# Half loads and an early split at the start, two reorderings in the MLP, and another inverse rms for the last rows, in a one-core transformer layer

## The chip, the cores and the metric

The kernel runs on one NeuronCore of a Trainium2 chip. Its engines are TensorE (PE, matrix products, with a separate weight load PEld), VectorE (DVE), ScalarE (ACT), GpSimd (POOL) and SyncE (SP), which issues the DMAs. Each engine works through its own instruction stream in order; semaphores tie them together. The metric is the device time in microseconds, lower is better. Before the change it is 1483.99 us (median of three runs, 1483.71 to 1484.88).

## The reference

One layer of an encoder on `x` of 1024 tokens by 1024 features, in float32. Each sub-layer is normalised on the way in and on the way out and added to the residual.

```
h = rmsnorm(x, g_mix_pre);  proj = h @ w_in
y = concat(rmsnorm(forgetting_attention(fq, fk, fv, f_logit)),
           rmsnorm(chunked_relpos_attention(cq, ck, cv, rel_bias)))     # 8 + 8 heads of 64
x = x + rmsnorm(y @ w_out, g_mix_post)
x = x + rmsnorm(memory_cross_attention(rmsnorm(x), rmsnorm(mem)), g_mem_post)   # 4 heads, 256 memory tokens
y = square(relu(rmsnorm(x, g_ff_pre) @ w_ff1)) @ w_ff2                  # hidden 4096
out = x + rmsnorm(y, g_ff_post)
rmsnorm(x, g) = x * rsqrt(mean(x*x) + 1e-6) * g
```

## The kernel before

Every float32 product is made of three products of fp32r parts: each operand is split into `hi` (a copy in fp32r, by ACT) and `lo` (the rest, by DVE or POOL), and `mm3` (lines 193 to 195) issues hi.hi, lo.hi and hi.lo into one PSUM bank. So an operand is ready for PE only when both parts are, and the second and third products wait for the lo parts.

**Start** (from line 1368, an order written out by hand). `xT` is the transposed input in pairs of 128-row slices; slice kc of 8 is scaled by the gain into `hT[0]` (`gained`: ACT makes hi, DVE makes lo). Two value weights are loaded in parts and split: weight 1 (`w1`, 256 columns, two parts of 4 slices) and weight 0 (`w0`, 264 columns, three parts of 3, 3 and 2). `wraw` has three buffers, so a fourth weight part waits for the first to be split. PE first runs 30 transposes of the identity as a warm-up, then 8 slices of weight 1 for four banks (96 matmuls: slice kc of all four banks, then the next kc), then eight small matmuls `ssx` that sum squares over the features, then blocks of weight 0, one bank at a time (24 matmuls each). `square` makes the squares on ACT and adds them on DVE. For the other half of the tokens ACT squares whole rows of `x` (`row_squares`). POOL takes the inverse roots by `pow` (`rcols`), and PE broadcasts them by the transposes `rr`. The order of the loads is that of SP's instruction stream.

**Attention and cross-attention** are ordered by a planner (`Flow`) with costs and due times; the change does not touch it.

**MLP** (from line 1700, again in a hand-written order). Both products are done as one level of a seven-product scheme (Strassen, Winograd's form). In the first half each j of 16 has the products `px`, `pz`, `px` again, `pv`, `pz` again; the weight sums for j + 1 are made on POOL (`nxt.sums`) and split on ACT and DVE (`nxt.split`). `g22` (line 1948) reads the bank `pz`, which the fifth product adds into, so PE waits there until DVE has made g22. `sums` (the function that line 1975 defines) squares and adds the results of one j and stores them to `gd` in DRAM. In the second half there are seven products n = 0 to 6 of 8 steps k each; `fetch(s)` loads the rows of step s, `prepare(s)` splits them (and, for some products, first adds or subtracts weights), and `multiply` runs 24 matmuls a step for four row blocks. The banks are X (n = 0, 2, 4, 6) and Y (n = 1, 3, 5). `gather` moves them to the row accumulators `yc`. After n = 4 ACT copies X to the first half of rows 4 to 7, and after n = 6 DVE subtracts the new X from it.

**End.** The last three steps of n = 6 run one row block at a time: `gather`, `squares` (ACT sums the squares of the half row; DVE multiplies by the gain), `inverse` (POOL: sum, then `pow`), and `finish` (DVE: scale and add the residual, in two halves, each stored by SP).

Of the kernel before, what the change touches and what calls it, by code (L numbers as in the profile page):

```python
# [14 lines left out]
F32 = mybir.dt.float32  # L15
# [120 lines left out]
def build(ctx, tc, nc, out, t):  # L136
# [127 lines left out]
    def load_pair(th, p):  # L264
# [3 lines left out]
        nc.sync.dma_start(xt, t["xT"][th, p])  # L268
        return xt
# [17 lines left out]
    def value_weights(g, raws=None, only=None):  # L287

        n = 264 if g == 0 else 256
        src = t["w_v0"] if g == 0 else t["w_v1"]  # L290
        raws = [] if raws is None else raws
        for i, (a, b) in enumerate(((0, 3), (3, 6), (6, 8)) if g == 0 else ((0, 4), (4, 8))):
            if only in (None, i):
                raw = wp.tile([P, b - a, n], F32, tag="wraw", bufs=3, name=f"wrawv{g}{a}")
                nc.sync.dma_start(raw, src[:, a:b, :])
                raws.append(raw)
        return raws

    def value_split(g, raw, i, pieces=1):
# [6 lines left out]
        for j in range(0, k, n):  # L306
            nc.scalar.activation(wh[:, j:j + n, :], raw[:, j:j + n, :], AF.Copy)
            nc.vector.tensor_sub(wl[:, j:j + n, :], raw[:, j:j + n, :], f(wh[:, j:j + n, :]))
        return [(wh[:, j, :], wl[:, j, :]) for j in range(k)]
# [1060 lines left out]
    with tc.manual_schedule():  # L1370
        xT = {0: [load_pair(0, 0)], 1: []}
        gmix = const.tile([P, KC], F32, name="gmix")
        nc.sync.dma_start(gmix, t["g_mix_pre"])
        raw1 = value_weights(1, None, 0)
        xT[0] += [load_pair(0, 1), load_pair(0, 2)]
        value_weights(1, raw1, 1)
        xT[0].append(load_pair(0, 3))
        raw0 = value_weights(0, None, 0)
        vs = {g: value_tiles(g) for g in (1, 0)}
        warm = mm_tile([P, 4, P], "warm", "tr")  # L1380
        for n in range(30):
            nc.tensor.transpose(warm[:, n % 4, :], ident, ident)

        def gained(kc):

            x, g, dh = xT[0][kc // 2][:, kc % 2, :], gmix[:, kc:kc + 1], hT[0].hi(kc)
            nc.scalar.activation(dh, x, AF.Copy, scale=g)
            nc.vector.scalar_tensor_tensor(hT[0].lo(kc), x, g, f(dh), op0=ALU.mult, op1=ALU.subtract)
# [11 lines left out]
        for kc in (0, 1):  # L1400
            gained(kc)
        w1 += value_split(1, raw1[0], 0, 2)
# [26 lines left out]
        w0 += value_split(0, raw0[1], 1)  # L1429
        nc.vector.tensor_scalar(rcols[0], ps, EPS, None, op0=ALU.add)  # L1430
        nc.gpsimd.tensor_tensor(rcols[0], rcols[0], mhalf[:, 0:4], op=ALU.pow)
        w0 += value_split(0, raw0[2], 2)

        def row(b):
            xr.append(p1.tile([P, D], F32, tag="sp", bufs=5, name=f"x{b}"))
            nc.sync.dma_start(xr[-1], t["x"][b * P:(b + 1) * P, :])
# [7 lines left out]
        for b in range(4, TB):  # L1444
            row(b)
        for p in range(4):
            xT[1].append(load_pair(1, p))
        ps0 = [values(0, w0, 0, "s")]
        for b in (4, 5):
            row_squares(b)  # L1450
        for kb in range(4):
            value_leave(1, kb, first[kb])
        for b in (6, 7):
            row_squares(b)
# [421 lines left out]
    def prepare(s):  # L1876
# [19 lines left out]
        elif name in ("T3", "T4"):  # L1896
            nc.vector.tensor_sub(rb, t2b[k], rb)
        nc.scalar.activation(ah, ra, AF.Copy)  # L1898
# [8 lines left out]
    with manual:  # L1907
        sums = lambda: None
        for j in range(NP):
# [38 lines left out]
            nc.vector.tensor_add(g22, z, u3)  # L1948
            if after:
# [37 lines left out]
        sums()  # L1987


        pfs.close()  # L1990
# [183 lines left out]
```

## Time and profile before

| | |
|---|---|
| median of the runs | 1483.99 us (1483.71 to 1484.88) |
| profiled execution, its own time | 1484.06 us |
| its span in the trace | 1482.3 us |
| PE busy | 1466.0 us, 99% |
| DVE, ACT, POOL busy | 948.6, 797.3, 391.3 us |
| DMA | 220.67 MB, mean 149 GB/s |
| granted TensorE clock, mean | 0.999 |

A row of a timeline gives start, length (both in us), engine, line, operation, what is written and read, the shape and the count; the bracket at its end is the time that the engine was idle before it and what ended that. A row of the waits names who waited for whom, the total in us, how often, and the longest. A row of a group has the count, then the busy time in us and the mean length of one in ns. A row of a DMA issue has its size and the time from issue to landing.

### The profile page before, as it was taken

What the parts mean: (1) busy time and instruction counts of PE and PEld (TensorE: products, weight loads), DVE (VectorE), ACT (ScalarE), POOL (GpSimd) and SP (SyncE); (2) the same over time, 40 slices, a digit from 0 to 9 for tenths busy, and PEclk for the clock granted to TensorE, in tenths of its full rate; (3) what the DMA queues carried; (4) which work ended last, traced back from release to release, by engine and by line L of the source; (5) the groups of instructions that cost most, each with busy time, mean ns of one, the idle gap of its engine ahead of it and who ended that gap; (6) DMA issues with size and microseconds to landing.
All of it is one profiled execution on the core that took longest, in us unless ns stands there. A gap on an engine that the chain in (4) does not pass through costs nothing. (4 is left out here: it accounts for less than half of the span.)

```text
span 1482.3 us, 21601 instructions
## 1 busy us (share of the span) xinstructions
PE 1466.0 (99%) x7606; PEld 1250.3 (84%) x7606; DVE 948.6 (64%) x1644; ACT 797.3 (54%) x1417; POOL 391.3 (26%) x613
## 2 busy tenths in 40 slices
PE   8999999999999999999999999999999999999998
PEld 8989888888889988888888887888888888888886
DVE  6777667565576835974384687675444665656577
ACT  6567567465567835553353455555555453443542
POOL 0144355353344200531041413432222000000021
PEclk9999999999999999999999999999999999999999
DMA  7133322522315552461251447674445785445565
GB/s 271 48 87 79 82 67 70 150 67 60 79 58 149 176 178 85 154 202 58 89 182 43 153 146 241 235 243 148 155 150 170 250 346 178 142 139 202 178 247 199
DMA packets 83484, 220.67 MB, mean 149 GB/s; under 512 B 10008, under 2 KB 14112, under 8 KB 83376
## 3 DMA queue, kind: packets, MB, share of 16 engines
q1 hardware_dynamic: 83376, 219.30, 44.6%
q8 instruction: 60, 0.98, 0.3%
q14 instruction: 48, 0.39, 0.1%
HBM read 159.96 MB, written 50.91 MB: 142 GB/s over the span
## 5 line engine op out<-in xcount | busy, mean ns | idle before, releaser
L700 DVE TENSOR_TENSOR pl<-ptr,ph 128x512 fp32r<-128x512 f32 (+1 forms) x152 | 92.2, 616 | 39.5 <-ACT ph L703 34.8
L1898 ACT ACTIVATE whif<-ra 128x1024 fp32r<-128x1024 f32 x37 | 39.2, 1061 | 122.1 <-PE fy L194 62.6
L1900 DVE TENSOR_TENSOR wlof<-ra,whif 128x1024 fp32r<-128x1024 f32 x37 | 45.3, 1225 | 91.2 <-ACT whif L1898 91.2
L703 ACT ACTIVATE ph<-ptr 128x512 fp32r<-128x512 f32 (+1 forms) x152 | 79.1, 539 | 39.4 <-PE ptr L694 32.9
L2014 POOL TENSOR_SCALAR rf<-sf 128x1 f32<-128x1 f32 x8 | 8.2, 1028 | 326.6 <-ACT jf L1999 326.3
L731 PE MATMUL pv<-ph,vs 128*128 128x256 f32 x304 | 79.6, 286 | 0.0
L732 PE MATMUL pv<-pl,vs 128*128 128x256 f32 x304 | 78.6, 283 | 0.3 <-DVE pl L700 0.3
L193 PE MATMUL fx<-vhif,whif 128*128 128x512 f32 x168 | 65.4, 389 | 0.0
L194 PE MATMUL fx<-vlof,whif 128*128 128x512 f32 x168 | 65.4, 389 | 0.0
L195 PE MATMUL fx<-vhif,wlof 128*128 128x512 f32 x168 | 65.4, 389 | 0.0
L732 PEld LDWEIGHTS pv<-pl,vs 128*128 128x128 f32 x304 | 57.6, 189 | 4.6 <-POOL pl L689 0.5
L731 PEld LDWEIGHTS pv<-ph,vs 128*128 128x128 f32 x304 | 57.3, 189 | 4.1
L1788 POOL TENSOR_TENSOR sc<-wf,wf 128x512 f32<-128x512 f32 x14 | 20.1, 1437 | 144.0 <-DMA wf<-in_w_ff 89.3
L193 PE MATMUL k<-hT_hi,whik 128*128 128x512 f32 x128 | 52.5, 411 | 0.0
L193 PE MATMUL mq<-h2T_hi,whimq 128*128 128x512 f32 x128 | 51.5, 403 | 0.0
L193 PE MATMUL q<-hT_hi,whiq 128*128 128x512 f32 x128 | 50.9, 398 | 0.0
L193 PE MATMUL ym<-whimo,oT_hi 128*128 128x512 f32 x128 | 50.3, 394 | 0.1
L194 PE MATMUL k<-hT_lo,whik 128*128 128x512 f32 x128 | 50.2, 393 | 0.0
L193 PE MATMUL yw<-whiwo,yT_hi 128*128 128x512 f32 x128 | 50.2, 392 | 0.0
L195 PE MATMUL k<-hT_hi,wlok 128*128 128x512 f32 x128 | 50.1, 392 | 0.0
L194 PE MATMUL q<-hT_lo,whiq 128*128 128x512 f32 x128 | 50.1, 391 | 0.0
L195 PE MATMUL mq<-h2T_hi,wlomq 128*128 128x512 f32 x128 | 50.1, 391 | 0.0
(606 smaller groups left out, 5027.1 us busy)
## 6 DMA issues: line engine op xcount, KB each, us to landing
ra<-gd SPq DMA_DIRECT2D x56, 512.0 KB, 3.9
wg<-in_w_ff SPq DMA_DIRECT2D x56, 512.0 KB, 5.9
wf<-in_w_ff SPq DMA_DIRECT2D x38, 512.0 KB, 4.0
gd<-s SPq DMA_DIRECT2D x48, 256.0 KB, 2.1
wrawmq<-in_w_mq SPq DMA_DIRECT2D x16, 512.0 KB, 3.8
wrawmo<-in_w_mo SPq DMA_DIRECT2D x16, 512.0 KB, 3.8
gd<-u SPq DMA_DIRECT2D x32, 256.0 KB, 2.1
gd<-g SPq DMA_DIRECT2D x25, 256.0 KB, 2.5
```

Source lines behind the costliest of these rows:

```text
L193: nc.tensor.matmul(ps, lh, rh, start=start, stop=False, skip_group_check=more)
L194: nc.tensor.matmul(ps, lh, rl, start=False, stop=False, skip_group_check=more)
L195: nc.tensor.matmul(ps, ll, rh, start=False, stop=stop, skip_group_check=more)
L700: flow.put("V", at, 0.7, lambda: nc.vector.tensor_sub(pl[:, live, :], tr[:, live, :], f(ph[:, live, :])), done)
L703: flow.put("S", flow.end, 0.6, lambda ph=ph, tr=tr, live=live: nc.scalar.activation(ph[:, live, :], tr[:, live, :], AF.Copy), split)
L731: nc.tensor.matmul(pv, v, ph[:, hs, :], start=c == 0 and half == 0, stop=False)
L732: nc.tensor.matmul(pv, v, pl[:, hs, :], start=False, stop=c + 1 == len(steps) and half == 1)
L1788: eng.tensor_sub(sc[:, k1], r0[:, k0], r1[:, k0])
L1898: nc.scalar.activation(ah, ra, AF.Copy)
L1900: nc.vector.tensor_sub(al, ra, f(ah))
L2014: nc.gpsimd.tensor_scalar(r, ssf[b][:, 0:1], ssf[b][:, 1:2], EPS, op0=ALU.add, op1=ALU.add)
```

## The change

- The first pair of `xT` and the first part of weight 1 are loaded in halves, in the order x half, gain, weight half, x half, weight half. A one-element activation (`early`) stands first on ACT, and the warm-up has 20 transposes in place of 30.
- The first part of weight 1 gets its hi parts from POOL; between its two halves stand the lo of slice 0 and both parts of slice 1.
- Weight 0's middle part gets a buffer of its own (tag `bias`); its last part is loaded behind rows 4 and 5 of `x`. Its first block is multiplied ahead of `ssx`, its middle split comes ahead of the last two squares, and all four row squares come ahead of the evictions of weight 1.
- The two value weights lie in DRAM part by part, so that a partition's values of one part are together.
- In the MLP's first half, for j = 0, the split of the next `s23` goes behind `g22`. `prepare(2)` goes ahead of the last `sums`, and these come at step 2 of the second half, behind `prepare(3)` and `prepare(4)`.
- T4's operands are swapped, and product 6 adds into the banks of products 0, 2 and 4; the copies and subtractions that this needed go. `squares` reads the bank.
- For row block 7, ACT takes a root q of the sum a (e = second half's sum + eps as its bias), and DVE makes 1 / (a / q + q), with a factor 2 in the gain. Its stores go out in two queues, 64 rows each (SP and ACT).

The core of the diff:

```diff
-        xT = {0: [load_pair(0, 0)], 1: []}
+        early = const.tile([P, 1], F32, name="early")
+        nc.scalar.activation(early, mhalf[:, 0:1], AF.Copy)
+        xt, xloads = load_pair(0, 0, True)
+        raw, wloads = value_raw(1, 0, halves=True)
+        xT, raw1 = {0: [xt], 1: []}, [raw]
         gmix = const.tile([P, KC], F32, name="gmix")
+        xloads[0]()
         nc.sync.dma_start(gmix, t["g_mix_pre"])
-        raw1 = value_weights(1, None, 0)
+        wloads[0]()
+        xloads[1]()
+        wloads[1]()
         xT[0] += [load_pair(0, 1), load_pair(0, 2)]
...
-        for n in range(30):
+        for n in range(20):
...
-        for kc in (0, 1):
-            gained(kc)
-        w1 += value_split(1, raw1[0], 0, 2)
+        gained_hi(0)
+        w1 += value_split(1, raw1[0], 0, 2, lambda: (gained_lo(0), gained(1)))
...
@@ value_split
+            if between:
+                nc.gpsimd.tensor_copy(wh[:, j:j + n, :], raw[:, j:j + n, :])
+            else:
+                nc.scalar.activation(wh[:, j:j + n, :], raw[:, j:j + n, :], AF.Copy)
             nc.vector.tensor_sub(wl[:, j:j + n, :], raw[:, j:j + n, :], f(wh[:, j:j + n, :]))
+            if between and j == 0:
+                between()
...
-        value_weights(0, raw0, 1)
-        value_weights(0, raw0, 2)
+        raw0 += [value_raw(0, 1, "bias"), None]
         for kc in (4, 5):
             square(kc)
         w0 += value_split(0, raw0[0], 0)
+        w0 += value_split(0, raw0[1], 1)
         for kc in (6, 7):
             square(kc)
+        for b in (4, 5):
+            row(b)
+        raw0[2] = value_raw(0, 2)
+        w0 += value_split(0, raw0[2], 2)
+        ps0 = [values(0, w0, 0, "s")]
...
@@ first half of the MLP
-                nxt.split("s23")
+                if j:
+                    nxt.split("s23")
...
             nc.vector.tensor_add(g22, z, u3)
+            if more and not j:
+                nxt.split("s23")
...
@@ between the halves
-        sums()
-        pfs.close()
+        prepare(2)
...
-                if s + 2 < len(steps):
+                if 0 < s < len(steps) - 2:
                     prepare(s + 2)
+                if s == 2:
+                    sums()
+                    pfs.close()
...
-                multiply(banks, range(4), [s], n in (2, 4, 5))
+                multiply(banks, range(4), [s], n in (2, 4, 5, 6))
...
@@ the last rows
+        def inverse_last(b):
+            a, q, r = (small.tile([P, 1], F32, tag="rstd", bufs=8, name=f"{k}f{b}") for k in "aqr")
+            e = small.tile([P, 1], F32, tag="rstd", bufs=8, name=f"ef{b}")
+            nc.vector.tensor_scalar(e, ssf[b][:, 1:2], EPS, None, op0=ALU.add)
+            nc.scalar.activation(q, e, AF.Sqrt)
+            yield
+            nc.scalar.activation(q, ssf[b][:, 0:1], AF.Sqrt, bias=e)
+            nc.gpsimd.tensor_scalar(a, ssf[b][:, 0:1], ssf[b][:, 1:2], EPS, op0=ALU.add, op1=ALU.add)
+            nc.vector.reciprocal(r, q)
+            nc.vector.scalar_tensor_tensor(q, a, r, q, op0=ALU.mult, op1=ALU.add)
+            nc.vector.reciprocal(r, q)
+            rf[b] = r
+            yield
...
-                nc.sync.dma_start(out[b * P:(b + 1) * P, cs], xts[b][:, cs])
+                if b < TB - 1:
+                    nc.sync.dma_start(out[b * P:(b + 1) * P, cs], xts[b][:, cs])
+                    continue
+                for i, queue in enumerate((nc.sync, nc.scalar)):
+                    r = slice(i * P // 2, (i + 1) * P // 2)
+                    queue.dma_start(out[b * P:(b + 1) * P, cs][r, :], xts[b][r, cs])
...
         for tp in range(4):
-            multiply(X, [tp], range(len(steps) - 3, len(steps)), False)
+            multiply(X, [tp], range(len(steps) - 3, len(steps)), True)
             if tp:
                 finish(tp + 3)
-            gather(6, tp, X[tp])
-            squares(tp + 4, 0, True)
-            inverse(tp + 4)
+            if tp == 3:
+                next(last)
+            squares(tp + 4, 0, X[tp])
+            if tp < 3:
+                inverse(tp + 4)
+        next(last)
         finish(7)
```

More of the change, by code (lines that the diff above doesn't have):

```diff
@@ L262, in build, with load_pair @@
     hT = [Act(f"hT{h}") for h in range(2)]
-    def load_pair(th, p):
+    def load_pair(th, p, halves=False):
         tag = "sp" if th else "klo"
         xt = p1.tile([P, 2, HT], F32, tag=tag, bufs=5 if th else 4, name=f"xT{th}{p}")
-        nc.sync.dma_start(xt, t["xT"][th, p])
-        return xt
+        if not halves:
+            nc.sync.dma_start(xt, t["xT"][th, p])
+            return xt
+        return xt, [lambda j=j: nc.sync.dma_start(xt[:, j, :], t["xT"][th, p][:, j, :]) for j in (0, 1)]
     rows = []
@@ L285, in build, with value_raw, value_split @@
     fcol = p1.tile([P, TB, 8], F32, tag="o2", bufs=2, name="fcol")
[L287 to L299, printed above, removed]
+    VPARTS = {1: ((0, 4), (4, 8)), 0: ((0, 3), (3, 6), (6, 8))}
+    def value_raw(g, i, tag=None, halves=False):
+        n, (a, b) = 264 if g == 0 else 256, VPARTS[g][i]
+        shape = [P, b - a, n]
+        raw = (wp.tile(shape, F32, tag="wraw", bufs=3, name=f"wrawv{g}{a}") if tag is None else
+               p1.tile(shape, F32, tag=tag, bufs=2, name=f"wrawv{g}{a}"))
+        src = t[f"w_v{g}"][a * P * n:b * P * n].rearrange("(p k n) -> p k n", p=P, n=n)
+        if not halves:
+            nc.sync.dma_start(raw, src)
+            return raw
+        h = (b - a) // 2
+        return raw, [lambda j=j: nc.sync.dma_start(raw[:, j:j + h, :], src[:, j:j + h, :]) for j in (0, h)]
+    def value_split(g, raw, i, pieces=1, between=None):
         k, shape = raw.shape[1], list(raw.shape)
@@ L1442, in row_squares @@
             nc.scalar.activation(junk, xr[b - 4], AF.Square, scale=1.0 / 32.0, accum_out=ss1[:, b - 4:b - 3])
-        for b in range(4, TB):
+        for b in (6, 7):
             row(b)
@@ L2129, in blocks, with parts @@
         return a(w.reshape(KC, P, -1, P).transpose(2, 1, 0, 3))
-    def rows(w):
-        return a(w.reshape(KC, P, -1).transpose(1, 0, 2))
+    def parts(w, ranges):
+        w = w.reshape(KC, P, -1)
+        return a(np.concatenate([w[x:y].transpose(1, 0, 2).reshape(-1) for x, y in ranges]))
     w = i["w_in"][0]
```

59 lines of the change are left out of this document (31 added, 28 removed).

## The prediction

> **What bounds the kernel now.** I read the page first (share of each engine), then the list of what TensorE (PE) waited for, then the timelines around those waits, and the last microseconds.
>
> ```profile
> span 1482.3 us, 21601 instructions
> PE 1466.0 (99%) x7606; PEld 1250.3 (84%) x7606; DVE 948.6 (64%) x1644; ACT 797.3 (54%) x1417; POOL 391.3 (26%) x613
> ```
>
> PE is busy for all but 16.3 us of the span, and the change leaves its arithmetic alone. What can be won lies in those 16 us; what can be lost is a new wait. The waits:
>
> ```profile
> PE v L193 <- ACT whiv L307: 2.7, 1, 2.7
> PE pz L193 <- DVE g L1948: 1.2, 1, 1.2
> PE rr L1464 <- POOL rx L1456: 1.0, 1, 1.0
> PE fx L194 <- DVE bl L1901: 0.7, 1, 0.7
> PE ssx L1428 <- DVE sqx L1397: 0.4, 1, 0.4
> ```
>
> The other long piece is the time after the last matmul. The diff touches each of these places, so I price three stretches: start, middle, end.
>
> **Start: half loads, first split on GpSimd (POOL).**
>
> ```profile
> 1.34 5.20 PE L1382 MATMUL warm<-ident 128*128 128x128 f32 x30 [1.34 <-POOL ident masks.py:199]
> 4.50 1.28 ACT L1387 ACT_TABLE_LOAD   x1 [4.50 <-DMA gmix<-in_g_mix_pre]
> 8.57 1.15 ACT L307 ACTIVATE whiv<-wrawv 128x512 fp32r<-128x512 f32 x2 [1.45 <-DMA wrawv<-in_w_v]
> 9.87 1.34 ACT L1387 ACTIVATE hT_hi<-xT,gmix 128x512 fp32r<-128x512 f32 x2
> 10.20 0.28 PE L195 MATMUL v<-whiv,hT_lo 128*128 128x256 f32 x1
> 14.23 1.29 DVE L308 TENSOR_TENSOR wlov<-wrawv,whiv 128x512 fp32r<-128x512 f32 x2
> 21.36 0.28 PE L195 MATMUL v<-whiv,hT_lo 128*128 128x256 f32 x1
> ```
>
> The first value phase has 96 matmuls (8 slices kc, 4 banks, 3 products). The third starts at 10.20 and the last at 21.36: 93 steps in 11.16 us, 0.12 each, with no gap. It starts late because the first value weight lands at about 8.5; ScalarE (ACT) then splits it.
>
> After the change a quarter as many bytes must land before the first multiplication can have both operands: half of x, the gain, half of the weight. That half weight lands somewhere between 4.5 (when gmix, issued before it, has landed) and 8.5 (when the whole one lands now). POOL's copy of 128x512 is not in this trace; the nearest row with one large input is wider, and its length is my price:
>
> ```profile
> L632 POOL TENSOR_SCALAR spc1g<-spc1g,smc1g 128x640 f32<-128x640 f32 x4 | 3.2, 802 | 4.9 <-DVE smc1g L631 4.8
> L436 POOL TENSOR_TENSOR wloq<-wrawq,whiq 128x512 fp32r<-128x512 f32 x16 | 20.6, 1308 | 34.6 <-ACT whiq L427 34.5
> ```
>
> So 0.8, upper end 1.3 (two inputs), lower end the 0.58 of one ACT copy (1.15 for two). Landing at 5.0 plus 0.1 plus 0.8, then VectorE (DVE) 0.69 for the low part and 0.75 for hT_lo(0): the third matmul would start near 7.3 instead of 10.2. The table load moves ahead of all this (the tiny "early" activation), and hides. Ten warm-up transposes fewer end PE's warm-up near 5.0 to 5.6; they cost nothing, as PE then waits anyway.
>
> But the gain is capped by the next load. xT1 is the whole second pair, behind the same bytes as now:
>
> ```profile
> 2.10 0.91 SPq L268 DMA_DIRECT2D xT<-in_xT  x2
> ...
> xT<-in_xT SPq DMA_DIRECT2D x1, 512.0 KB, 7.8
> wrawv<-in_w_v SPq DMA_DIRECT2D x1, 512.0 KB, 9.4
> wrawv<-in_w_v SPq DMA_DIRECT2D x1, 396.0 KB, 10.4
> ```
>
> Issued at 2.10, it lands 7.8 later, at 9.9, and ACT begins hT_hi(2) at 9.87 already now. From there ACT's and DVE's orders are unchanged as far as the low part of weight kc 4, which is ready at 14.23 + 0.69 = 14.92. PE's 50th matmul (first low product of kc 4) cannot start before 14.95; now it starts at 10.20 + 47 x 0.12 = 15.84. So the phase ends 0.9 earlier, not 2.9: it moves to the last matmul at 20.5.
>
> Second weight: its middle part gets the free "bias" buffer, so it loads at once; its last part goes behind two rows of x. The last two wrawv rows land at 3.04 + 9.4 and 4.32 + 10.4, so about 0.4 MB per us; the middle part lands near 15.7, two rows near 18.3, the last part near 19, before DVE wants it at 22.8. In the DVE order the two squares additions now follow the middle split:
>
> ```profile
> 20.45 1.48 DVE L1397 TENSOR_TENSOR sqx<-sqx,sqx 128x512 f32<-128x512 f32 x2
> 23.16 0.71 DVE L308 TENSOR_TENSOR wlov<-wrawv,whiv 128x528 fp32r<-128x528 f32 x1
> 23.33 1.43 POOL L1431 TENSOR_TENSOR rx<-rx,mhalf 128x4 f32<-128x4 f32 x1 [22.04 <-DVE rx L1430]
> 28.85 1.05 POOL L1456 TENSOR_TENSOR rx<-rx,mhalf 128x4 f32<-128x4 f32 x1
> 29.95 1.09 PE L1464 MATMUL rr<-ident,rx 128*128 128x128 f32 x8 [0.99 <-POOL rx L1456]
> ```
>
> DVE's work from 20.45 on is the same but for one tiny operation, so wlov's last part ends near 23.5. PE begins the second weight's first block at 20.6, reaches kc 6 at 22.8 and waits 0.7 there: a new stall in place of ssx's. The block ends at 24.1, ssx (eight small matmuls, priced like rr's, 1.0) at 25.1, the next block (24 x 0.12) at 28.0. POOL's roots keep their order: the first follows ssx as now, 25.5 to 26.9, the second one's addition and root to about 28.2 (ACT's four row squares, now ahead of the evictions, are in time). So rr starts near 28.25 instead of 29.95: **1.7 won**. Bounds: if the halves land no earlier than 8.5, the low part, hT_lo(0) and (1) and the other low part push DVE's chain 1.3 to 1.5 later and 0.2 stays; if xT1 too comes 1.4 earlier, 3.1. The four value evictions move behind rows 6 and 7's squares; PE needs their banks only after rr.
>
> **Middle: two reorderings.**
>
> ```profile
> 910.12 1.33 DVE L1586 TENSOR_TENSOR v1lo_s<-sc,v1hi_s 128x1024 fp32r<-128x1024 f32 x1 [4.91 <-ACT v1hi_s L1583]
> 912.09 0.69 DVE L1948 TENSOR_TENSOR g<-pz,u 128x512 f32<-128x512 f32 x1
> ...
> 908.59 0.39 PE L195 MATMUL px<-T_hi,v0lo_s 128*128 128x512 f32 x1
> 911.31 0.39 PE L195 MATMUL pv<-T_hi,wlo_s1a 128*128 128x512 f32 x1
> 912.93 0.47 PE L193 MATMUL pz<-B_hi,u0hi_s 128*128 128x512 f32 x1 [1.24 <-DVE g L1948]
> ```
>
> DVE sat 4.91 waiting for v1hi_s (late through its load and POOL) with g22's two operands behind it. px ends at 908.98; u and g22 need 0.7 each and would be done at 910.4, before PE asks for z at 911.54 (0.227 per matmul). Won: 912.93 - 911.54 = 1.4, and 0.1 in the two slow matmuls after it. v1lo_s moves to about 911.7; px of j = 1 would want it 12 matmuls later, at 914.3, so nothing new waits. The deferred instruction pair is ACT's and DVE's only; its sources' loads on SyncE (SP) stay.
>
> ```profile
> 1175.70 1.04 ACT L1898 ACTIVATE ah<-ra 128x1024 fp32r<-128x1024 f32 x1
> 1179.63 1.22 DVE L1901 TENSOR_TENSOR bl<-wg,bh 128x1024 fp32r<-128x1024 f32 x1
> 1179.79 0.39 PE L193 MATMUL fx<-bh,ah 128*128 128x512 f32 x1
> 1180.90 0.50 PE L194 MATMUL fx<-bl,ah 128*128 128x512 f32 x1 [0.73 <-DVE bl L1901]
> ```
>
> prepare(2) now goes ahead of the last sums; bl can follow ah, bh at about 1178 and is wanted at 1180.02. Won: 0.9, and 0.1 behind it. The sums (2 ACT, 4 DVE, 4 stores of gd_7) go behind prepare(3) and (4) on ACT and DVE, and on SP behind gfin's load and the fetches. What reads those rows of gd comes over 20 steps of 24 matmuls later, so nobody waits, and the loads that now stand ahead of them go out sooner. **2.5 together**; bounds 1.3 (one of them comes back at the next operand) and 2.6.
>
> **Signs and banks.** T4's operands swapped and the seventh product added into the same banks: four ACT copies and four DVE subtractions go. Only the last subtraction is on the path.
>
> **End.**
>
> ```profile
> 1475.04 0.69 DVE L2061 TENSOR_TENSOR yc<-yc,fx 128x512 f32<-128x512 f32 x1
> 1475.82 0.63 ACT L1999 ACTIVATE jf<-yc 128x512 bf16<-128x512 f32 x1 [3.36 <-DVE yc L2061]
> 1476.36 0.18 ACT L1999 ACTIVATION_READ_ACCUMULATOR jf<-yc 128x1 f32 x1
> 1477.62 0.75 DVE L2021 SCALAR_TENSOR_TENSOR xf<-yg,rf,xf 128x512 f32<-128x512 f32 x1 [1.17 <-POOL rf L2015]
> 1478.28 0.75 DVE L2021 SCALAR_TENSOR_TENSOR xf<-yc,rf,xf 128x512 f32<-128x512 f32 x1
> L1236 DVE RECIPROCAL mst<-mst 128x1 f32<-128x1 f32 x32 | 4.9, 157 | 4.2 <-ACT mp L1234 4.1
> ```
>
> Now 2.58 pass from the last matmul's end (about 1475.0, yc follows at once) to xf. Then: ACT squares straight from the bank, 0.72 with the read; a Sqrt of 128x1, priced like the read (0.18) plus 0.1; reciprocal, multiply-add, reciprocal at 0.157 + 0.03 each; handover 0.05. Sum 1.6, so 0.95 won. POOL's one sum lies beside the root. The span ends 3.9 after the first xf's end (1478.37), in which both stores of the row go out; the bytes stay the same, whichever queues issue them, so I take 0 for the two queues (bounds 0.3 lost by ACT's issue, 0.4 won). The Sqrt's table load is one, ahead of the last square, while PE runs the last block: that block is 18 matmuls, 4.1, so the square before it ends near 1471.6, the load near 1472.9, and the last square is wanted at 1475.0. [...]
>
> **Sum.** 1.7 + 2.5 + 0.95 = 5.15. The profiled execution took 1484.06 (span 1482.3, median of the runs 1483.99), so **1478.9**.
>
> **Rivals.**
> - No early landing: the half loads help nothing, because 4.5 to 8.5 is lost in the DMA engines whatever is queued. Start wins 0.2: 1480.4. For it: the weight now lands 6.9 after its issue, xT1 only 1.4 later. Chance 0.14.
> - Loads run ahead: xT1 comes too with less disturbance from the table load (4.50) on; start wins 3.1: 1477.5. Chance 0.14.
> - The middle does nothing: the waits on g22 and bl only move to the next operand, as the same DMAs feed them. 1481.4. Against it: the slack of 2.6 at px. Chance 0.10.
> - Table flips at the end: Square and Sqrt in different sets, a load before each, 2 x 1.28 on the path: 1481.5. The changed instruction stream shows one load. [...] Chance 0.03.
> - Slower: PE's clock. Twenty transposes end before PE is at speed, PE idles again, and the value matmuls run at half speed, 0.24 each. 43 such matmuls undo everything; all 96 and 20 more of the next block cost 13.9: 1492.8. Against it: the old gap of 2.7 us lost no speed. [...] Chance 0.04.
>
> **Numbers.** The forecast has 0.55, its own range 1477.2 to 1480.3. A measurement here tells 0.2% (2.97 us) from no change: below 1481.0 is faster, above 1487.0 slower. Forecast, first and second rival are faster (0.83, less 0.02 for their edges); the third, the fourth and those edges are within 0.2% (0.15); slower is the clock (0.04). Range 1476.5 to 1481.0: down to the second rival with the end's bound of 0.4 and 0.6 more, as xT1's landing is the softest number; up to where the third begins.
>
> **What would show it.** v's wait at 2.7 goes to PE starting near 6 to 7, then a gap ahead of kc 2 or kc 4; ssx free of waits, one near 0.7 on wlov's last part; rr near 28.3; no wait at pz (j = 0) or at step 2's bl; 1.6 from the last matmul to xf. Wrong would be: rr at 29.9 or later, the waits reappearing one product later, or a span that ends more than 3.9 after the first xf's end.

## The result and the profile after

The changed kernel takes 1480.69 us (median of nine runs, 1479.98 to 1481.45); the kernel before, run beside it, 1484.88 (nine runs, 1483.66 to 1486.85). The ratio is 0.9972, interval 0.9963 to 0.9982: faster by some 4 us where 5.15 were forecast. 1478.9 was predicted, and the range to 1481.0 holds the result. The profiled execution took 1479.98, and its span is 4.1 us shorter. All the times that follow are points in a trace, unless a median is named.

First the page of the kernel after, its first line and the busy line:

```profile
span 1478.2 us, 21594 instructions
PE 1466.9 (99%) x7596; PEld 1251.5 (85%) x7596; DVE 946.7 (64%) x1644; ACT 796.8 (54%) x1415; POOL 393.9 (27%) x614
```

Then what PE waited for in the kernel after (us in total, how often, the longest):

```profile
PE warm L1400 <- POOL ident masks.py:199: 1.3, 1, 1.3
PE sf4g L627 <- DVE mnf4g L631: 0.3, 2, 0.2
PE pv L743 <- DVE pl L711: 0.3, 1, 0.3
PE sf6g L627 <- DVE mnf6g L631: 0.2, 1, 0.2
PE px L195 <- DVE wlo_a L1611: 0.2, 1, 0.2
```

The five waits quoted from before (v 2.7, pz 1.2, rr 1.0, fx 0.7, ssx 0.4) are gone from the list; nothing of size stands in their place. (Part of that at the start is a slower PE: its first value products, 0.21 apart to 10.6 and 0.12 from there, are taken up further down.) The timeline of the kernel after at the points that the prediction named:

```profile
5.13 0.61 POOL L314 CAST whiv<-wrawv 128x512 fp32r<-128x512 f32 x1 [3.83 <-DMA wrawv<-in_w_v]
7.18 0.58 PE L195 MATMUL v<-whiv,hT_lo 128*128 128x256 f32 x1
8.73 1.34 ACT L1419 ACTIVATE hT_hi<-xT,gmix 128x512 fp32r<-128x512 f32 x2 [2.26 <-DMA xT<-in_xT]
21.61 0.70 DVE L317 TENSOR_TENSOR wlov<-wrawv,whiv 128x528 fp32r<-128x528 f32 x1
26.88 1.09 PE L1489 MATMUL rr<-ident,rx 128*128 128x128 f32 x8
...
907.39 0.69 DVE L1977 TENSOR_TENSOR g<-pz,u 128x512 f32<-128x512 f32 x1
909.18 0.39 PE L193 MATMUL pz<-B_hi,u0hi_s 128*128 128x512 f32 x1
...
1173.08 1.23 DVE L1929 TENSOR_TENSOR bl<-wg,bh 128x1024 fp32r<-128x1024 f32 x1
1175.99 0.39 PE L194 MATMUL fx<-bl,ah 128*128 128x512 f32 x1
...
1469.56 0.39 PE L195 MATMUL fx<-bh,al 128*128 128x512 f32 x1
```

rr comes at 26.88 (29.95 before): 3.07 ahead. That lead shrinks to 2.70 by 892 us and to 2.36 at the wait on wlo_a just behind. g is ready at 908.08 and pz starts at 909.18 without a wait (912.93 before: 3.75 ahead). bl is ready at 1174.31, 1.7 before PE asks for it (1175.99 against 1180.90: 4.91 ahead), and the last matmul starts 5.05 earlier, at 1469.56 against 1474.61. From there to the end of the span it was 7.69 us and is now 8.64: **the end loses 0.95, where it was to win 0.95**. Two rows of the end of the kernel before, to compare:

```profile
1474.61 0.39 PE L195 MATMUL fx<-bh,al 128*128 128x512 f32 x1
1475.76 0.69 DVE L2001 TENSOR_TENSOR yg<-yc,gfin 128x512 f32<-128x512 f32 x1
```

The end of the kernel after, in its timeline:

```profile
1469.07 0.15 DVE L2056 TENSOR_SCALAR ef<-sf 128x1 f32<-128x1 f32 x1
1469.30 1.28 ACT L2057 ACT_TABLE_LOAD   x1 [2.64 <-DVE ef L2056]
1470.59 0.20 ACT L2057 ACTIVATE qf<-ef 128x1 f32<-128x1 f32 x1
1470.70 0.58 ACT L2029 ACTIVATE jf<-fx 128x512 bf16<-128x512 f32 x1
1471.40 0.30 ACT L2059 ACTIVATE qf<-sf,ef 128x1 f32<-128x1 f32 x1
1471.40 0.69 DVE L2035 SCALAR_TENSOR_TENSOR yg<-fx,gfin 128x512 f32<-128x512 f32 x1 [2.18 <-ACT jf L2029]
1472.01 0.15 DVE L2061 RECIPROCAL rf<-qf 128x1 f32<-128x1 f32 x1
1472.72 0.75 DVE L2071 SCALAR_TENSOR_TENSOR xf<-yg,rf,xf 128x512 f32<-128x512 f32 x1
1473.50 1.40 ACTq L2078 DMA_DIRECT2D out_y<-xf  x2
```

Three things are to be seen. ACT stood idle for 2.64 us and then began the table load at 1469.30, not while it was idle but once DVE had made ef, the operand of the first root. So the load ran past the last matmul (its end 1469.95) and the last square jf began at 1470.70, 0.75 late. DVE's yg, which now reads the same bank as jf, began only when ACT was done, and the reciprocal stands behind it on DVE. In the kernel before, where both read yc, they ran side by side (1475.76 and 1475.82). And the first xf ends at 1473.47, but the span ends 4.73 later, where it was 3.9 before.

### The profile page after: what moved, and what is told of

Its sections match the earlier page's. It is cut to its first block, busy times and chain, and to the rows that moved or that the text cites. A ratio compares the mean times of both kernels' runs of the same rounds, so it can differ in the third digit from the quotient of the medians.

```text
span 1478.2 us, 21594 instructions
## 1 busy us (share of the span) xinstructions
PE 1466.9 (99%) x7596; PEld 1251.5 (85%) x7596; DVE 946.7 (64%) x1644; ACT 796.8 (54%) x1415; POOL 393.9 (27%) x614
## 5 line engine op out<-in xcount | busy, mean ns | idle before, releaser
L194 PE MATMUL mq<-h2T_lo,whimq 128*128 128x512 f32 x128 | 50.1, 391 | 0.0
```

Of the source, the lines that this page charges most:

```text
L194: nc.tensor.matmul(ps, lh, rl, start=False, stop=False, skip_group_check=more)
```

## The experiments

Each time in the table is a median, with its ratio to the kernel before as run beside it (its medians lay between 1484.0 and 1484.9). The other columns are points of one profile each. "xT1" is when ACT starts on the second x pair; "tail" runs from the last matmul's start to the end of the span; as the span is given to 0.1 us, a tail is good to 0.05.

| kernel | median (runs) | ratio, interval | xT1 | rr | last matmul | tail |
|---|---|---|---|---|---|---|
| before | 1484.88 (9) | | 9.87 | 29.95 | 1474.61 | 7.69 |
| after | 1480.69 (9) | 0.9972 [0.9963, 0.9982] | 8.73 | 26.88 | 1469.56 | 8.64 |
| early table load | 1479.97 (8) | 0.9974 [0.9964, 0.9985] | 8.39 | 26.52 | 1469.27 | 7.93 |
| one store queue | 1479.16 (6) | 0.9967 [0.9956, 0.9979] | 9.04 | 27.17 | 1470.18 | 7.62 |
| both | 1479.29 (5) | 0.9966 [0.9954, 0.9979] | 9.96 | 28.10 | 1471.07 | 6.93 |
| old inverse, one queue | 1478.68 (4) | 0.9963 [0.9950, 0.9977] | 9.64 | 27.76 | 1470.44 | 6.76 |
| before + end | 1485.40 (11) | 1.0010 [1.0001, 1.0019] | 8.47 | 28.56 | 1473.41 | 8.59 |
| before + start | 1481.51 (10) | 0.9981 [0.9972, 0.9991] | 9.79 | 27.91 | 1472.79 | 7.51 |
| before + middle | 1482.21 (10) | 0.9987 [0.9977, 0.9996] | 9.92 | 30.58 | 1472.73 | 7.67 |
| 30 transposes | 1480.37 (10) | 0.9978 [0.9969, 0.9987] | 9.68 | 27.82 | 1470.56 | 8.64 |
| whole loads | 1483.17 (10) | 0.9994 [0.9985, 1.0003] | 7.81 | 27.98 | 1470.82 | 8.78 |
| whole loads, 34 transposes | 1481.69 (11) | 0.9983 [0.9974, 0.9992] | 8.85 | 28.17 | 1471.82 | 8.78 |
| late first table | 1480.15 (7) | 0.9971 [0.9960, 0.9981] | 9.58 | 27.73 | 1470.38 | 8.32 |
| old inverse, whole loads, 34 | 1480.35 (10) | 0.9973 [0.9964, 0.9982] | 9.25 | 28.61 | 1471.83 | 6.77 |

### The end: table load, store queues, inverse

**The load moved into the idle time.** A root of block 6's sum, which nothing reads, goes behind block 6's square, so that the table is loaded while ACT has nothing to do.

```diff
             squares(tp + 4, 0, X[tp])
+            if tp == 2:
+                pre = small.tile([P, 1], F32, tag="rstd", bufs=8, name="pre")
+                nc.scalar.activation(pre, ssf[6][:, 0:1], AF.Sqrt)
```

> The changed kernel with one more tiny root on ScalarE, of row block 6's first sum, right behind that block's squares, so that the table load no longer stands behind the wait for DVE's ef. Theory (the exposed load is the larger loss of the end): the load lies beside PE's last block, the last square starts within 0.1 us of the last matmul's end instead of 0.75 after it, and from the last matmul's start to the span's end 7.9 pass instead of 8.64; about 1480.0. Rival (the end is slow because ACT and DVE read one bank in turn and the small DVE steps take long): the last square starts earlier, but xf does not, and the end stays at 8.5 or more.

**One store queue.** The last rows are stored whole by SP.

```diff
-                if b < TB - 1:
-                    nc.sync.dma_start(out[b * P:(b + 1) * P, cs], xts[b][:, cs])
-                    continue
-                for i, queue in enumerate((nc.sync, nc.scalar)):
-                    r = slice(i * P // 2, (i + 1) * P // 2)
-                    queue.dma_start(out[b * P:(b + 1) * P, cs][r, :], xts[b][r, cs])
+                nc.sync.dma_start(out[b * P:(b + 1) * P, cs], xts[b][:, cs])
```

> The changed kernel with the last row's two stores whole, by SP alone. Theory (two queues lengthen the stores): from the end of the first xf to the span's end 3.9 us as before the change instead of 4.73, so 0.8 less; about 1479.9. Rival (the longer end is another effect, for example a later start of the data): still 4.6 to 4.8.

**Both edits together**, as shown.

> Both mendings together: early table load and one queue. Theory: the two add, 7.1 from the last matmul's start to the span's end, 0.6 less than before the change (7.69); about 1479.2, ratio to before near 0.9962. Rival (they overlap, as the store stream is bound elsewhere): no better than the better one of the two.

The tail goes from 8.64 to 7.93 with the early load (0.71), to 7.62 with one queue (1.02) and to 6.93 with both (1.71): two independent costs that add up. The timeline of the kernel with the early load shows the last square 0.03 behind the last matmul's end, and what then follows:

```profile
1469.27 0.39 PE L195 MATMUL fx<-bh,al 128*128 128x512 f32 x1
1469.69 0.60 ACT L2029 ACTIVATE jf<-fx 128x512 bf16<-128x512 f32 x1 [0.48 <-PE fx L195]
1470.41 0.69 DVE L2035 SCALAR_TENSOR_TENSOR yg<-fx,gfin 128x512 f32<-128x512 f32 x1 [1.50 <-ACT jf L2029]
1471.02 0.15 DVE L2061 RECIPROCAL rf<-qf 128x1 f32<-128x1 f32 x1
1471.73 0.75 DVE L2071 SCALAR_TENSOR_TENSOR xf<-yg,rf,xf 128x512 f32<-128x512 f32 x1
```

From the last matmul's end (1469.66) to xf are 2.07 us even so, where 1.6 was forecast. The root beside yg ends at 1470.70, but the reciprocal starts at 1471.02, as yg has DVE until then: 0.32. The three small operations take 0.71 from the first start to xf, where 0.56 was counted: 0.15.

The stores, as the profile's DMA view has them for the last 5.2 us of the kernel after (GB/s in 40 slices of 0.13 us, then the issues with KB each and us to landing):

```profile
GB/s 0 0 0 0 0 0 0 0 0 0 0 0 110 221 173 189 236 126 378 441 363 410 347 174 378 236 142 95 16 0 0 0 0 0 0 0 0 0 0 0
out_y<-xf SPq DMA_DIRECT2D x2, 128.0 KB, 2.3
out_y<-xf ACTq DMA_DIRECT2D x2, 128.0 KB, 2.7
```

And for the last 3.8 us of the kernel with one queue (a slice is 0.095 us here):

```profile
GB/s 0 0 0 0 0 0 0 0 0 108 280 410 366 345 431 302 388 345 474 410 366 388 345 388 173 0 0 0 0 0 0 0 0 0 0 0 0 0 0 0
out_y<-xf SPq DMA_DIRECT2D x2, 256.0 KB, 2.0
```

The same bytes go at 280 to 474 GB/s almost at once with one queue. With two, the first six slices move 110 to 236, and the last four tail off from 236. A store of half the size takes longer to land, 2.3 and 2.7 against 2.0. From the end of the first xf to the end of the span, the seven profiles with two queues show 4.4 to 4.9 us, those with one queue 3.7 to 3.9. So it is shown that this way of storing is slower. A split other than by 64 rows each was not tried.

**The old inverse.** The changed kernel with one queue, and with POOL's sum and `pow` again for block 7 (its gain without the factor 2); the banks are still read without the subtraction. Beside the edit for the queue:

```diff
-        last = inverse_last(7)
...
-            if tp == 3:
-                next(last)
             squares(tp + 4, 0, X[tp])
-            if tp < 3:
-                inverse(tp + 4)
-        next(last)
+            inverse(tp + 4)
```

> The changed kernel with the last row's inverse rms as before (POOL's sum and pow), gain without the factor 2 and one queue; the bank sums stay. Theory: no table load, no root; the square starts at once, and the end is the old one less the subtraction (0.72): 7.69 - 0.72 = 7.0; about 1479.1, as good as both mendings of the new way, so that root and reciprocals win under 0.2. Rival (root and reciprocals win 0.4 or more against pow, once their load is hidden): 7.3 or more here.

Its timeline, from the last matmul on:

```profile
1470.44 0.39 PE L195 MATMUL fx<-bh,al 128*128 128x512 f32 x1
1470.93 0.60 ACT L2029 ACTIVATE jf<-fx 128x512 bf16<-128x512 f32 x1 [3.39 <-PE fx L195]
1472.10 0.56 POOL L2046 TENSOR_TENSOR rf<-rf,mhalf 128x1 f32<-128x1 f32 x1
1472.69 0.75 DVE L2068 SCALAR_TENSOR_TENSOR xf<-yg,rf,xf 128x512 f32<-128x512 f32 x1 [0.35 <-POOL rf L2046]
```

From the last matmul's end to xf are 1.86 us, 0.2 less than by roots with the load hidden: yg runs beside POOL's sum and power, so it costs nothing here. The tail is 6.76, the shortest, and the median 1478.68 the lowest of all. So of the end's edits, dropping the subtraction is the one that wins: from the last matmul's end to xf it was 2.62 and is 1.86, 0.76 less. The other 0.17 of the 0.93 between the tails lies behind the first xf (3.9 before, 3.74 here) and is there in the kernel before with the start alone too (3.74, tail 7.51), so it does not come from the bank; its cause is open. The new inverse and the two queues lose the 0.93 twice over.

**The kernel before with the end alone** (T4's sign, the seventh product in the banks, the new inverse, two queues).

```diff
-                multiply(banks, range(4), [s], n in (2, 4, 5))
+                multiply(banks, range(4), [s], n in (2, 4, 5, 6))
...
+        last = inverse_last(7)
...
```

> The kernel before with the end of the change alone: T4's sign, the seventh product added into the banks, the last row's inverse by roots and reciprocals, and its store in two queues; loads, start and the two reorderings as before. By the prediction 0.95 us is won: ratio 0.9994, tail from the last matmul's start 6.7. By the theory drawn from the trace of the change (the root's table load waits with its operand and stands ahead of the last square, and the two-queue store takes 0.8 to 1.0 longer): tail 8.6, start and middle as before, so 0.9 us is lost, ratio 1.0006. If the removed copies and subtractions in the steps before matter to PE, the last matmul comes earlier than 1474.6 by some tenths.

Tail 8.59, ratio 1.0010 with the interval just above 1: the end alone makes the kernel a little slower. Its start and middle keep the old waits (v 1.5, rr 1.0, fx 0.8, pz 0.7). That its last matmul nonetheless comes at 1473.41 is its early xT1 (8.47), not the change: it is 1.39 ahead of the kernel before at rr already and 1.20 at the last matmul, so the copies and subtractions that go win PE nothing ahead of the tail.

### The start: what bounds it

**The start alone, on the kernel before** (half loads, early split, 20 transposes, the order of weight 0).

```diff
+        xt, xloads = load_pair(0, 0, True)
+        raw, wloads = value_raw(1, 0, halves=True)
...
-        for n in range(30):
+        for n in range(20):
```

> The kernel before with the start's edits alone (loads, split on POOL, order, DRAM layout of the value weights, 20 transposes). Theory: rr starts near 26.9 as in the changed kernel, 3.05 earlier; the last matmul 2.4 to 3.0 earlier, as some of it is lost by 900 us; about 1482.2, ratio 0.998. Rival (the drift between 30 and 900 us eats it, because DVE and the loads bound long stretches there): under 1.5 left at the last matmul.

Ratio 0.9981, and the old waits at pz and at bl come back in it, 0.7 and 0.9. rr comes at 27.91, not 26.9, as xT1 is there at 9.79 only; the last matmul is 1.82 earlier than before, short of the 2.4 to 3.0 of the theory and above the rival's 1.5.

**30 transposes** in the changed kernel.

```diff
-        for n in range(20):
+        for n in range(30):
```

> The changed kernel with 30 warm-up transposes again. In the changed kernel's trace the first value matmuls run 0.213 apart until about 10.7, then 0.12. Theory (20 transposes end too early to bring PE to speed, and this costs little because DVE's last low part of weight 0 is the bound behind it): value matmuls run 0.12 apart from the start, the first phase ends up to 1 us earlier, PE then waits near 1 us on wlov, and rr starts within 0.3 of 26.9; time within 0.5 of 1480.7. Rival 1 (the half speed costs 1.4 in full): rr near 25.5. Rival 2 (speed comes by PE's clock phase, not by the transposes): still 0.213 apart after about 5 us.

**Whole first loads** in the changed kernel, in the old order, all else as changed.

```diff
-        xt, xloads = load_pair(0, 0, True)
-        raw, wloads = value_raw(1, 0, halves=True)
+        xt = load_pair(0, 0)
         gmix = const.tile([P, KC], F32, name="gmix")
-        xloads[0]()
         nc.sync.dma_start(gmix, t["g_mix_pre"])
-        wloads[0]()
-        xloads[1]()
-        wloads[1]()
+        raw = value_raw(1, 0)
```

> The changed kernel with the first pair of x and the first weight part loaded whole again, in the old order (x, gain, weight); all else as changed. Theory (the early table load, not the halves, lets xT1 land at 8.7 instead of 9.9): xT1 still lands near 8.7, the first matmul comes near 7.5 to 8.5 instead of 5.8, and rr near 27 to 27.5, so the halves are worth under 0.6. Rival (the halves do it): xT1 near 9.9, rr near 28.3.

**Whole loads and 34 transposes**, so that the warm-up runs into the values: the edit before this one, and

```diff
-        for n in range(20):
+        for n in range(34):
```

> The changed kernel with the first x pair and the first value weight loaded whole, in the order of the kernel before, and 34 warm-up transposes instead of 20. Whole loads with 20 transposes let the second x pair land at 7.81 us, the earliest so far, yet rr came at 27.98, 20.2 us behind it, where every kernel with half loads needed 18.1. Theory A (PE's clock took that back: PE paused between the warm-up and the values, and the granted clock showed 0.50 from 8.0 to 11.3): with 34 transposes the warm-up runs into the values, no half clock follows, rr comes 18.1 to 18.5 us behind the landing, near 26.2, and the span is some 1.6 us shorter than with whole loads and 20 transposes, 1478.0 against 1479.6. Theory B (whole loads cost the 2 us themselves, because the first weight's low part comes later on DVE): rr stays some 20 us behind the landing, near 28, with the clock at 1.00. If the landing itself slips back to 9 to 10, the distance from landing to rr still tells the two apart.

**The first table load late**: the `early` activation is taken out.

```diff
-        early = const.tile([P, 1], F32, name="early")
-        nc.scalar.activation(early, mhalf[:, 0:1], AF.Copy)
```

> The changed kernel without the tiny early activation: ACT's first table load then waits for the gain to land. If the load only stands beside the landings (theory: xT1's landing decides, and varies from execution to execution between 8.4 and 10.0): ACT's first gained half starts 1.3 us later, near 5.0, the first value product some 0.5 later at most, and rr still 18.1 us behind the start of the third gained half; time within 0.1% of the changed kernel. Rival (the load's own traffic delays whatever is landing, so that the early load is what let xT1 land at 8.7): xT1 lands near 9.9 as before, rr near 28, 1.2 us slower.

In all eight kernels with half loads, rr comes 18.12 to 18.15 us after ACT starts on xT1, whatever the warm-up, the table load or the clock; in the old order it is 20.08 (before), 20.09 and 20.66. So with half loads the landing of xT1 sets the start. The forecasts of rr near 26.9 (30 transposes) and of 27 to 27.5 (whole loads) missed: it came at 27.82 and at 27.98, the first with xT1 at 9.68, the second although xT1 was there at 7.81, which neither the theory nor its rival had.

That landing itself wanders between 7.8 and 10.0 from kernel to kernel: 8.4 to 10.0 with half loads, 7.8 to 9.9 without. Five of these kernels differ in their end alone (after, early table load, one queue, both, old inverse) and span 8.39 to 9.96, so the 1.1 by which xT1 came earlier in the profile after is a draw. The one profile without the early table load (9.58) lies inside that stretch: no effect of that load is seen. Nor is one of the half loads on xT1.

The fair comparison is a profile of nearly the landing of before (9.96 for 9.87), that of the kernel with both end edits, in its timeline:

```profile
9.96 1.33 ACT L1419 ACTIVATE hT_hi<-xT,gmix 128x512 fp32r<-128x512 f32 x2 [2.57 <-DMA xT<-in_xT]
10.71 1.41 DVE L1422 SCALAR_TENSOR_TENSOR hT_lo<-xT,gmix,hT_hi 128x512 fp32r<-128x512 f32 x2 [0.65 <-ACT hT_hi L1419]
22.83 0.70 DVE L317 TENSOR_TENSOR wlov<-wrawv,whiv 128x528 fp32r<-128x528 f32 x1
28.10 1.09 PE L1489 MATMUL rr<-ident,rx 128*128 128x128 f32 x8
```

rr comes at 28.10, 1.85 earlier than 29.95; 28.25 was predicted. Counted from xT1 it is 1.94 (20.08 less 18.14). Two rows of the kernel before say where that is won:

```profile
9.23 1.29 DVE L308 TENSOR_TENSOR wlov<-wrawv,whiv 128x512 fp32r<-128x512 f32 x2 [1.27 <-ACT whiv L307]
10.63 1.41 DVE L1388 SCALAR_TENSOR_TENSOR hT_lo<-xT,gmix,hT_hi 128x512 fp32r<-128x512 f32 x2
```

Before the change, from DVE's first work on xT1 to the start of the last low part are 12.53 us (10.63 to 23.16), and from there to rr 6.79. In the kernel with both end edits they are 12.12 and 5.27. So 0.41 is DVE's new order, and 1.52 is what follows the last low part, where the first block of weight 0 now stands ahead of ssx and rr no longer waits for POOL. DVE had its first two low parts behind it before xT1 in the old kernel too (9.23 + 1.29 = 10.52). So what the half loads and the split on POOL add to the new order is not shown: the new order with the old whole loads and the first split on ACT was not run. An estimate from the rows of before: its last product of weight 1 starts at 21.36, and the 24 of the next block, 0.12 apart, would have the last one start at 24.24; in the kernel with both end edits it starts at 24.18. By that estimate the halves and the early split add some 0.1 at this landing.

Once POOL has the split, whole loads do cost, through DVE's work. The kernel with whole loads and 34 transposes:

```profile
8.23 1.07 DVE L317 TENSOR_TENSOR wlov<-wrawv,whiv 128x512 fp32r<-128x512 f32 x1 [7.32 <-POOL whiv L314]
22.90 0.70 DVE L317 TENSOR_TENSOR wlov<-wrawv,whiv 128x528 fp32r<-128x528 f32 x1
28.17 1.08 PE L1485 MATMUL rr<-ident,rx 128*128 128x128 f32 x8
```

From the first low part to the last are 14.67 us of DVE without a gap, and rr follows 5.27 behind the last one's start, as in the kernel after (21.61 to 26.88). With half loads DVE has done the two first low parts and two hT_lo before xT1 is there, and only 12.1 us of the chain lie behind it. From xT1 to rr are 19.32 here, between the 18.1 to 18.5 of theory A and the 20 of theory B, with value products 0.12 apart in the rows from 21.76 on: 1.2 more than with half loads. So theory B has the cause right. But theory A has a share: with 20 transposes the same chain ran from 6.98 to 21.66, and rr came at 27.98, 6.32 behind, not 5.27. There PE was late, as its clock in the stretches of that kernel shows (PE's granted clock is the number before the last two):

```profile
7.00:8.00 1.00, 0.38 (x1) 0.19 (x1) 1.00 (x2) 0.19 (x1) 0.51 (x1) 0.99 0.96 356
8.00:9.00 1.00, 0.81 (x2) 0.52 (x3) 1.00 (x3) 1.00 (x2) 0.00 (x0) 0.50 0.99 401
11.00:12.00 1.00, 1.00 (x9) 1.00 (x8) 1.00 (x3) 1.00 (x3) 0.00 (x0) 0.80 1.02 403
```

The medians agree: whole loads with 20 transposes have the ratio 0.9994, and its interval does not meet that of the changed kernel (0.9985 to 1.0003 against 0.9963 to 0.9982); with 34 transposes (0.9983) the two intervals overlap.

### The middle alone, on the kernel before

```diff
-                nxt.split("s23")
+                if j:
+                    nxt.split("s23")
...
+            if more and not j:
+                nxt.split("s23")
...
-        sums()
-        pfs.close()
+        prepare(2)
...
```

> The kernel before with the two reorderings of the MLP alone (split of s23 behind g22 for j = 0; prepare(2) ahead of the last sums, these at step 2). Theory: they add to the rest: no wait at pz and at fx, last matmul 2.5 earlier (1.5 and 1.0), about 1482.4. Rival (they only worked because PE came earlier to them): less than 1.5.

Its offset to the kernel before goes from 0.74 behind at 896 us (0.63 of it was there at rr) to 0.68 ahead at pz, so 1.4 is won there, and to 1.71 ahead at the second half's step 2: another 1.0. Both waits are absent from its list. Its last matmul is 1.88 earlier than before, as it was 0.63 late at rr; without that it is the 2.5 of the theory. The ratio is 0.9987.

### A version to beat both

The old inverse and one queue with whole loads and 34 transposes: four of the edits shown above, and nothing else.

```diff
-        last = inverse_last(7)
...
-                for i, queue in enumerate((nc.sync, nc.scalar)):
...
-        xt, xloads = load_pair(0, 0, True)
+        xt = load_pair(0, 0)
...
-        for n in range(20):
+        for n in range(34):
```

> The candidate to beat both: the last row's inverse, root and store as before the change (a sum and a power on POOL, one store queue, with the seventh product still added into the banks), whole first loads and 34 transposes, all else as changed. If the landing decides the start and the clock is kept (theory A): rr near 26.2 and a tail of 6.8 from the last matmul's start, so a span near 1475.8 and a time near 1477.3, ratio 0.995. If whole loads lose whatever the warm-up (theory B): rr near 28, time near 1478.8, no better than the old last row with half loads (1478.68).

Its tail is 6.77, but rr comes at 28.61, and the median of 1480.35 is no better than the 1478.68 of the old inverse with half loads (the intervals of the two ratios overlap). That kernel keeps the lowest median: the change without its new inverse and without its second queue. Against the changed kernel its gain is read from the tail (8.64 to 6.76) and the medians; here too the intervals overlap.

## Why the prediction was right, and where its terms were off

The verdict, faster by some 0.3%, and the range were right; the sum was so by terms that partly cancelled. In the profile after, 1.1 us of an early landing, which is luck, stand against an end that is 1.9 worse than forecast. What the medians owe to the landing is not known, as one execution of each kernel has a trace. By medians the start alone wins 2.6, the middle alone 1.9, and the end alone loses 0.9: 3.5 together, against 4.2 for the whole change, which agrees within the intervals.

- **Start, 1.7 forecast.** The profile shows 3.07. Of it 1.85 is the new order at an equal landing, so the cap by xT1, DVE's chain and the length behind it were read rightly; the rest is the landing, 8.73 for 9.9. That bound was named (3.1 if the loads run ahead), but the cause given for it, the earlier table load, is not seen: without that load xT1 comes at 9.58, inside the spread of the kernels that have it. How much of the 1.85 comes from the halves is not shown; by the estimate above nearly all of it is the order of weight 0, ssx and the row squares. POOL's copy took 0.61, not 0.8; the third matmul started at 7.18 (7.3 forecast).
- **The stall of 0.7 on the last low part.** PE loses 0.5 there in four profiles (early table load, 30 transposes, late first table, before + start), less in two (both, old inverse), and in the profile after no wait is listed. The gap that was named ahead of kc 2 or kc 4 shows in the profiles of the early table load (13.49) and of 30 transposes (14.78), 0.7 each. In the profile after PE ran its first value products 0.21 apart in place of 0.12 and so came to both places later; that this hid the waits is argued from the rows.
- **Middle, 2.5 forecast.** Measured 1.4 + 1.0 alone on the kernel before; inside the change the lead grows from 2.36 to 5.05. The slack read at px was real, and nothing that was moved back waited.
- **End, 0.95 forecast, 0.95 lost.** The step that failed is "The Sqrt's table load is one, ahead of the last square, while PE runs the last block". It is one, but it begins only when the operand of its root is there (ef at 1469.07, the load at 1469.30); 0.70. Then "ACT squares straight from the bank" left out that yg reads the same bank: DVE waits for ACT's square, and the reciprocal stands behind yg, 0.32 (in the two traces yg waits for jf only where both read the bank; that the bank is the cause was not tested by itself); the small operations 0.15 more. Last, "I take 0 for the two queues" (bounds 0.3 lost, 0.4 won): 0.8 to 1.0 lost, outside the bounds. What did win, 0.76, is the subtraction that goes. The sum 0.70 + 0.32 + 0.15 + 0.8 is 1.97, against the 1.90 between forecast and profile.
- **The lead of 3.07 at rr is 2.36 behind 893 us.** Some 0.4 goes gradually between 100 and 500 us, and 0.34 at the wait on wlo_a (0.2 in the list above, with longer products beside it). The kernel before with the start alone loses 0.5 over the same 400 us, the one with the end alone nothing, so the gradual loss goes with the new start; why stays open. No term stood for it.
- **The rival of PE's clock** came true in its first half: with 20 transposes the profile after has value products 0.21 apart to about 10.6, and those of one queue and of whole loads have a granted clock of 0.50 from 9 to 11. With 30, the kernel before and the one with the end alone show 0.12 from the third product on, and with 34 the old inverse with whole loads shows it from the fourth on. How far the number of transposes decides it is not shown: before + middle, with 30, came to rr 0.63 later than before, although DVE's rows up to 21.89 lie within 0.05 of those of before. In the profile after, rows of the values' timeline:

```profile
7.56 0.42 PE L193 MATMUL v<-whiv,hT_hi 128*128 128x256 f32 x1
7.78 0.41 PE L194 MATMUL v<-wlov,hT_hi 128*128 128x256 f32 x1
...
10.75 0.28 PE L193 MATMUL v<-whiv,hT_hi 128*128 128x256 f32 x1
10.86 0.28 PE L194 MATMUL v<-wlov,hT_hi 128*128 128x256 f32 x1
```

0.213 apart to about 10.6 and 0.12 from there, with a granted clock of 1.00 in each us from 7 to 12. It cost nothing, because DVE's chain behind xT1 is later than PE: 30 transposes move neither the 18.14 from landing to rr nor, beyond the interval, the time. With whole loads, where xT1 was there at 7.81 and DVE's chain came earlier, it did cost 1.05.

## What to carry to other kernels

A function's table load came here with the wait of the instruction that needs it (2.64 us on ef): if it is to hide, give it an instruction of its own whose operand is long there, at a place where ACT is idle (0.71 of the tail here). Before an operation is moved to another engine to shorten a chain, look at what else reads the same bank, and at what stands in front of the chain's next step on its engine (here yg, which waited for jf and then held DVE 0.32 longer than the root took). And where a start depends on a landing that wanders by 1.5 us between profiles of the same start, compare profiles from that landing on, not from zero. A faster landing is worth its price only if something behind it waits for it: here, by the estimate above, the order of the work behind the second landing won nearly all of what the start won.

## What the runs showed of the hardware

- **The table load** took 1.28 us and the next activation followed 0.01 later: 1469.30 + 1.28, then 1470.59 in the profile after, and 1468.18 + 1.28, then 1469.47 in that of both end edits. After it, a root, a square and a root ran in turn without another load (1470.59, 1470.70, 1471.40), so the rival of the table flips is out.
- **Two store queues of 64 rows each** moved the last rows slower than one queue of 128: 110 to 236 GB/s in their first 0.8 us, against 280 to 474 behind a first slice of 108, and their stores landed after 2.3 and 2.7 us, against 2.0. In the middle of the same stores stand slices of 347 to 441 GB/s, the level of the one queue. What it is in the split that costs the time is not shown.
- **PE's granted clock fell to 0.50 for some 3.4 us** in the profiles of two kernels with 20 transposes. In the kernel with whole loads PE idled 1.70 us ahead of its first value product at 7.00, and the granted clock was 0.50 from 8.0 to 11.4 (0.99 in the us before, 0.80 in the us from 11). That first product took 0.38 us, the next, at 8.11, 0.58: the speed was there and was lost, with PE idle for 1.70 and 0.72 and one product between. In the kernel with one queue the clock was 1.00 in the us from 7, 0.64 in that from 8, 0.50 in the next two, 0.65 in that from 11 and 1.00 again from 12: by these means, 0.50 from about 8.3 to 11.7. The length of the gap does not decide it: the kernel before idled 2.7 us and kept a clock of 1.00 and products 0.12 apart, the one with one queue lost it with no wait over 0.7. In the profile after no row before 10.6 shows the full speed, though the granted clock reads 1.00: 20 transposes took 4.53 us, 0.23 each, and the values follow 0.21 apart, where the kernel before ran 12 transposes in the us from 5.0. What decides it stays open.
- **DVE beside POOL.** With whole loads and 20 transposes DVE's first low part took 1.07 us (from 6.98) while POOL copied the weight's second half (busy 0.51 us of the us from 7), and the second 0.68 (from 9.30) with POOL idle. With 34 transposes they took 1.07 and 0.68 as well, and in the profile after, with half loads, 0.69 each. That POOL's copy is the cause was not tested by itself.
